# Moving the inverse of the 16-blocks and the decay chain of a gated DeltaNet branch, with new due times

## The chip, the cores and the metric

One core of one Trainium2 chip runs the whole program. The metric is the device time of one execution in microseconds (us); before the change the median of three runs is 1434.36 us (1434.13 to 1436.87). Five engines work side by side, each with an instruction queue of its own that runs in order: TensorE (PE in the profile; PEld is its weight load), VectorE (DVE), ScalarE (ACT), GpSimd (POOL) and SyncE (SP), which here only issues transfers.

## The reference

A trunk of two layers over 256 tokens of width 1024. Each layer has a mixing part with three branches, then a mixture of 32 experts:

```python
p = h @ w_in          # q,k,v of A and B; q,k,v,z and decay/beta of C; gates
ya = _global_gqa(...)             # rms norm, rotary, softmax attention, 8 heads
yb = _neighbourhood_attn(...)     # windowed attention, 4 heads
yc = _gdn_bidir(...)              # gated DeltaNet, 4 heads, forward and backward
mix = ga * (ya @ wa) + gb * (yb @ wb) + gc * (yc @ wc)
h = layernorm(alpha * h + mix @ w_out)
h = layernorm(alpha * h + moe(h))
```

Branch C convolves q, k and v along the tokens (5 taps), takes SiLU, and runs a chunked delta rule. Per chunk of 64 tokens:

```python
g = -exp(A_log) * softplus(a + dt_bias);  beta = sigmoid(b)
gc = cumsum(g);  decay = exp(gc_i - gc_j)
m = strict_lower(k_beta @ k.T) * decay
u, w = solve(m + I, [v * beta, k_beta * exp(gc)])   # unit triangular
# then a scan over the chunks with a state per head
```

## The kernel before

**Stages.** Each layer has a mixing part (`mixer`, about 0 to 260 and 714 to 967 us of the trace) and an expert part (`moe`). In mixing, weights come in units of 512 KB or less: SP loads a unit, ACT rounds it to its high half (uh), and VectorE, or POOL for the units listed in `POOL`, takes the low half (ul, "a cut", L189). Three products of halves stand for one exact product (`mm3`). `take` loads four to five units ahead and cuts three ahead. Expert weights come in slabs of 1 MB through the same SP queue; fifteen slots on the right side are shared with the tiles of the mixing part ("places" A to U, L147): a place that `free` gives back can take a slab. Seven more slots and one open on the left when the mixer's own tiles are gone.

**Order.** TensorE's order in mixing is pinned to the order of the program text. The text runs `projections` (ga0, cqk, cz, cv, akv, aq, ga1, bqk, bv, gb0, gb1, gc0, gc1), then `merge` a, b, c, then `project`. Beside it run side lines (generators): `delta_line`, `key_line`, `query_line`, `attention_line`, `router_line`. A clock of the kernel's own adds a planned time for each product (`mm`, `tp`). After each step of a projection `pump` runs each line whose due time has come. A line that yields is due again after the next number of its list in `LAGS` (L46). So LAGS alone decides where in TensorE's order the steps of a line stand. The order on the other engines is left to the tile framework's scheduler, except where `high_priority`, `manual_schedule` or `issue_after` binds it.

**The delta line** (L626 to L971). Step one computes gates: tanh of z into szg, beta, and the decay chain that gives g (`sc`, `sb`; L636 to L669, a softplus by a series), then three products R of g with triangles on POOL (L678), then convolution 2. After a lag of 15.03, step two: sums of g on TensorE into bank eb, their exponents ev, factors nbe and kds, and the three decay differences db with exponents E (L683 to L709). Then turned q and k (qk, L720), their norms with `rsqrt` (a first step on VectorE, a power on POOL, L238), turned v (vt), products kT, qdT, and the grams (gr, L778) from which VectorE makes Z and qk. The diagonal 16-blocks of Z are gathered into Zc (L797, L799), written to DRAM and read back as Zd with one block per partition (L804, L806). The inverse of each block takes 15 steps of two instructions on POOL (L812 to L817), a transposing copy (L818), then goes back over DRAM (L821, L824) into Wc. Sixteen masked POOL products (L830) make block-diagonal X and Y. After a lag of 53.51, the doublings on TensorE: T (T16), X and Y (X16, Y16), T3, L. Then the scan of four steps: ks, vn, kv, ob, and at the end ycT.

**Convolution** `conv(i, b)` (L555): for two halves a centre tap (L561) and four shifted taps on VectorE, tanh on ACT, one product into cs[i]. `conv(0)` and `conv(1)` follow cqk, `conv(2)` stands in the delta line.

**Rotary** `norm_rope` (L571): a copy from PSUM (queries), squares on ACT, sums on VectorE, `rsqrt`, then x times the root, then two POOL products with the sines, one with the cosines and the sum on VectorE. `key_line` uses it with a lag of 10.0 before its transposes (kTA), `query_line` with 16.22 (qTA).

**Attention.** `attention_line` starts when keys and queries are done: scores (s_a), `softmax` (maxima, factors and scaling on VectorE, exponents on ACT), transposes (pT_a), values (o_a), four pairs of heads; then two pairs of branch B.

Names in the trace: a tile inside a place bears the place's name (placeB holds big8, cy1 and cs0; placeF big5 and big6, that is X and Y; placeJ Zc, Zd and tmp; placeS the small ones). gap holds kT, g, ev and the like. A line such as L164, L168, L173 is that of a helper (`tt`, `ts`, `stt`).

## Time and profile before

| what | us |
|---|---|
| median of three runs | 1434.36 |
| the profiled execution's own time | 1437.54 |
| its span, first to last instruction | 1435.9 |
| TensorE busy | 1349.3 |
| VectorE busy | 613.6 |
| ScalarE busy | 399.2 |
| POOL busy | 256.5 |

The profiled execution is 3.2 us above the median, 1.6 of it outside the span. Times in the rows further below count from the span's start. A row of a timeline has the start, the duration, engine, line and operation, the tiles (out<-in), the shapes, the count of merged instructions, and in brackets the engine's idle time before it and what ended it. Matmuls are pipelined and their ends are modelled, so starts are surer than ends. PEclk is the granted TensorE clock as a share of 2.4 GHz. The table's busy times are totals over stretches with different limits; what a part costs is read from its own stretch.

### The profile page before, as it was taken

Reading aid. Unit: us, or ns where it says so; the run is one execution under the profiler, and the core shown is the slowest. Engines: PE = TensorE matmul, PEld = TensorE weight load, DVE = VectorE, ACT = ScalarE, POOL = GpSimd, SP = SyncE. Lnnn points to the kernel's source line nnn. Section 1 sums busy time; section 2 is a strip of 40 time slices with the busy share of each in tenths; the row PEclk is TensorE's granted clock in tenths of the full one; section 3 lists DMA queues with packets and bytes.
Section 4 is the critical chain, followed back from the end, with each engine's and each line's share of the span. In section 5 each row is a group of like instructions: output and inputs, shape, how many; then the busy total and the mean of one; then the engine's idle time right before and its main releaser. Section 6 shows DMA issues by size and latency. Waiting matters only on the chain. (4 is left out here: it accounts for less than half of the span.)

```text
span 1435.9 us, 23914 instructions
## 1 busy us (share of the span) xinstructions
PE 1349.3 (94%) x9788; PEld 894.9 (62%) x9788; DVE 613.6 (43%) x1221; ACT 399.2 (28%) x761; POOL 256.5 (18%) x327
## 2 busy tenths in 40 slices
PE   8989999899998999999898899999999899999986
PEld 7867777555555555555487877875555555555532
DVE  6887567522221222222279866773222122222214
ACT  4445543221111211111235365332111111111111
POOL 4474303300000000000046661132000000000000
PEclk9989999999999999999999999999999999999998
DMA  7635779799999999999856466787999999999994
GB/s 233 211 113 139 249 252 341 278 409 418 419 419 414 419 419 419 419 419 420 352 153 194 122 194 232 282 348 287 419 419 418 418 420 419 419 419 419 418 419 189
DMA packets 114533, 479.89 MB, mean 334 GB/s; under 512 B 25168, under 2 KB 38000, under 8 KB 65520
## 3 DMA queue, kind: packets, MB, share of 16 engines
q1 hardware_dynamic: 112464, 471.85, 84.1%
q0 software_dynamic: 1376, 5.24, 1.0%
q8 instruction: 81, 1.33, 0.4%
q10 hardware_dynamic: 576, 1.18, 0.2%
q14 instruction: 36, 0.29, 0.1%
HBM read 476.40 MB, written 1.84 MB: 333 GB/s over the span
## 5 line engine op out<-in xcount | busy, mean ns | idle before, releaser
L179 PE MATMUL h<-w,h 128*64 128x256 f32 x2016 | 231.8, 386 | 22.6 <-PEq L1413 11.3
L179 PEld LDWEIGHTS h<-w,h 128*64 128x64 f32 x2016 | 143.9, 139 | 101.8 <-issue 16.9
L173 DVE SCALAR_TENSOR_TENSOR hid<-gate,h 128x256 f32<-128x256 f32 x64 | 26.9, 421 | 407.2 <-ACT gate L1504 407.2
L173 DVE SCALAR_TENSOR_TENSOR op<-mo,rt,op 64x512 fp32r<-64x512 f32 x128 | 96.0, 750 | 223.3 <-ACT op L1535 222.4
L1535 ACT ACTIVATE op<-mo,rt 64x512 fp32r<-64x512 f32 x128 | 87.4, 683 | 313.0 <-PE mo L179 273.5
L179 PE MATMUL mo<-w,hidT 128*64 128x512 f32 x720 | 167.8, 595 | 3.6 <-DMA w<-in_w_dram 1.6
L164 POOL TENSOR_TENSOR W<-P,rt 128x128 f32<-128x128 f32 x64 | 24.2, 398 | 779.1 <-PE PT L185 704.4
L1504 ACT ACTIVATE gate<-h 128x256 f32<-128x256 f32 x64 | 24.5, 384 | 408.3 <-PE h L179 408.3
L179 PEld LDWEIGHTS mo<-w,hidT 128*64 128x64 f32 x720 | 51.3, 137 | 92.2 <-issue 80.1
L179 PE MATMUL h<-w,xg 128*64 128x256 f32 x864 | 97.1, 381 | 3.8 <-ACT h L1478 2.4
L179 PE MATMUL h<-wl,h 128*64 128x256 f32 x768 | 86.3, 381 | 2.2 <-ACT h L1478 1.4
L179 PEld LDWEIGHTS h<-w,xg 128*64 128x64 f32 x864 | 60.9, 137 | 36.0 <-ACT h L1478 3.8
L179 PEld LDWEIGHTS h<-wl,h 128*64 128x64 f32 x768 | 53.9, 137 | 30.6 <-ACT h L1478 2.4
L179 PE MATMUL mo<-wl,hidT 128*64 128x512 f32 x304 | 70.1, 597 | 2.9 <-DMA wl<-in_w_dram 2.9
L179 PE MATMUL my<-op,PT 128*128 128x512 f32 x256 | 69.6, 411 | 0.4 <-DVE op L173 0.3
L179 PEld LDWEIGHTS my<-op,PT 128*128 128x128 f32 x256 | 45.6, 188 | 22.1 <-issue 12.4
L179 PE MATMUL xg<-P,hh 128*128 128x256 f32 x256 | 54.8, 294 | 0.0
L179 PEld LDWEIGHTS xg<-P,hh 128*128 128x128 f32 x256 | 39.1, 188 | 24.6 <-issue 24.4
L179 PE MATMUL h<-wl,xg 128*64 128x256 f32 x416 | 48.3, 382 | 5.2 <-DMA wl<-in_w_dram 3.6
L179 PE MATMUL xg<-P,hl 128*128 128x256 f32 x256 | 51.1, 281 | 0.0
L179 PEld LDWEIGHTS mo<-wl,hidT 128*64 128x64 f32 x304 | 20.6, 136 | 38.0 <-issue 32.4
L179 PEld LDWEIGHTS h<-wl,xg 128*64 128x64 f32 x416 | 28.6, 137 | 22.7 <-DMA wl<-in_w_dram 6.8
(459 smaller groups left out, 2456.7 us busy)
## 6 DMA issues: line engine op xcount, KB each, us to landing
w<-in_w_dram SPq DMA_DIRECT2D x268, 1024.0 KB, 19.9
wl<-in_w_dram SPq DMA_DIRECT2D x112, 1024.0 KB, 19.9
w_gb<-in_w_in_dram SPq DMA_DIRECT2D x16, 512.0 KB, 3.5
w_gc<-in_w_in_dram SPq DMA_DIRECT2D x16, 512.0 KB, 4.6
w_wo<-in_w_out_dram SPq DMA_DIRECT2D x16, 512.0 KB, 4.4
w_ga<-in_w_in_dram SPq DMA_DIRECT2D x14, 512.0 KB, 5.6
w_cqk<-in_w_in_dram SPq DMA_DIRECT2D x8, 512.0 KB, 3.5
w_aq<-in_w_in_dram SPq DMA_DIRECT2D x8, 512.0 KB, 4.9
```

The source lines that it names most:

```text
L164: return eng.tensor_tensor(out=o, in0=x, in1=y, op=op).ins
L173: return V.scalar_tensor_tensor(out=o, in0=x, scalar=s, in1=y, op0=op0, op1=op1)
L179: ins = T.matmul(o, l, r, start=start, stop=stop, skip_group_check=True).ins
L1504: A.activation(g, b[:, :256], AF.Tanh, scale=0.5)
L1535: A.activation(hi, src, AF.Copy, scale=w)
```

## The change

Decay chain: it reads its inputs from PSUM, has fewer instructions (factors folded), multiplies by a negated exp(A_log) made beforehand on POOL, and makes the two halves of g itself; gates and beta come after it. `conv(2)` is bound to be issued behind it. The centre tap of each convolution goes from VectorE to ACT. The exponents of eb are written twice, also to PSUM, for nbe and kds. Rotary: raw x is copied and turned on POOL, the root's first step goes to POOL, and the root multiplies last. cs[0] is written straight to kq, so its copy on POOL goes; places D and E swap their order. Diagonal blocks: one scaling and three multiply-adds through PSUM. The inverse goes to VectorE, in order behind the last cut on VectorE, after a new yield; its transposing copy to ACT; X takes four ACT instructions and Y one on VectorE. Lags: 53.51 becomes 12.0 (to the inverse) and 20.0 (to the doublings), keys 10.0 to 14.0, queries 16.22 to 20.5. Lines of context are left out below.

```diff
@@ -44,9 +44,9 @@
-    "delta": [15.03, 1.23, 3.7, 10.0, 0, 0.76, 53.51, 0, 0, 0.8, 0.24, 0.0, 0.52, 1.67, 1.37, 0, 2.87, 2.23, 0, 2.03, 1.99, 0, 2.87, 1.99, 0, 2.87, 6.3],
-    "key": [10.0],
-    "query": [16.22, 1.92, 1.92],
+    "delta": [15.03, 1.23, 3.7, 10.0, 0, 0.76, 12.0, 20.0, 0, 0, 0.8, 0.24, 0.0, 0.52, 1.67, 1.37, 0, 2.87, 2.23, 0, 2.03, 1.99, 0, 2.87, 1.99, 0, 2.87, 6.3],
+    "key": [14.0],
+    "query": [20.5, 1.92, 1.92],
@@ -145,8 +145,8 @@
-              "C": {"big7": 1024, "cs2": 512, "cs1": 512}, "D": {"kd": 1024, "kq": 1024},
-              "E": {"qA": 1024, "ub": 768}, "F": {"big5": 1024, "big6": 1024},
+              "C": {"big7": 1024, "cs2": 512, "cs1": 512}, "E": {"qA": 1024, "ub": 768}, "D": {"kd": 1024, "kq": 1024},
+              "F": {"big5": 1024, "big6": 1024},
@@ -235,10 +235,10 @@
-    def rsqrt(o, x, scale, eps, n):
+    def rsqrt(o, x, scale, eps, n, eng=V):
...
-            ts(V, o, x, scale, OP.mult, eps, OP.add)
+            ts(eng, o, x, scale, OP.mult, eps, OP.add)
@@ -294,6 +294,8 @@
+            if i not in POOL:
+                scope["cut"] = made[1]
@@ -550,7 +552,7 @@
-        cs = [of(f"cs{i}", 2, S) for i in range(3)]
+        cs = [kq[:, 1]] + [of(f"cs{i}", 2, S) for i in (1, 2)]
@@ -558,7 +560,7 @@
-                ts(V, y[:, m], bv[:, m], cw[:, ch, 2:3], OP.mult)
+                A.activation(y[:, m], bv[:, m], AF.Copy, scale=cw[:, ch, 2:3])
@@ -572,25 +574,23 @@
-            xv = x8(x[:, :n * 64])
-            raw = x8(b) if which else xv
-            if not which:
-                A.copy(x[:, :n * 64], b)
-            sq = y
-            A.activation(sq[:, :n * 64], b if which else x[:, :n * 64], AF.Square)
+            xv, yv = x8(x[:, :n * 64]), x8(y[:, :n * 64])
+            A.copy(x[:, :n * 64], b)
+            A.activation(dst, x8(b) if which else xv, AF.Square)
             rs = of(f"rs{t}", 8)
-            V.tensor_reduce(out=rs[:, :n], in_=x8(sq[:, :n * 64]), axis=AX.X, op=OP.add)
-            rsqrt(rs[:, :n], rs[:, :n], 1.0 / 64.0, 1e-6, n)
-            tt(V, xv, raw, rs[:, :n, None].to_broadcast([128, n, 64]), OP.mult)
-            yv = x8(y[:, :n * 64])
+            V.tensor_reduce(out=rs[:, :n], in_=dst, axis=AX.X, op=OP.add)
+            rsqrt(rs[:, :n], rs[:, :n], 1.0 / 64.0, 1e-6, n, G)
...
+
+            xv = x8(b) if which else xv
             tt(V, xv, xv, gc_[:, which, 0, t:t + 1].to_broadcast([128, n, 64]), OP.mult)
-            tt(V, dst, xv, yv, OP.add)
+            tt(V, xv, xv, yv, OP.add)
+            tt(V, dst, xv, rs[:, :n, None].to_broadcast([128, n, 64]), OP.mult)
@@ -626,47 +626,44 @@
-            ba = of("ba", 2, 2, 2, 4)
-            for t in range(2):
-                V.tensor_copy(ba[:, :, :, t], zb[t][:, 256:272].rearrange("p (a d h) -> p a d h", a=2, d=2))
-                A.activation(szg[:, t], zb[t][:, :256], AF.Tanh, scale=0.5)
-                stt(szg[:, t], szg[:, t], 1.0, zb[t][:, :256], OP.add, OP.mult)
-            tt(G, szg.rearrange("p t (h d) -> p (t h) d", d=64), szg.rearrange("p t (h d) -> p (t h) d", d=64),
-               gn[:, 2:3].to_broadcast([128, 8, 64]), OP.mult)
+
+            sb = bank("s", f"sb{l}")
+            rr, sq_, acc, th_ = (sb[:, 16 * i:16 * i + 16] for i in range(4))
+            by_t = lambda ap: ap.rearrange("p (d t h) -> p d t h", d=2, t=2)
+            by_d = lambda ap: ap.rearrange("p (d h) -> p d h", d=2)
             beta = of("beta", 2, 8)
-            A.activation(beta, ba[:, 0].rearrange("p d t h -> p d (t h)"), AF.Tanh, scale=0.5)
-            ts(V, beta, beta, 0.5, OP.mult, 0.5, OP.add)
             sc = of("gsc", 8, 16)
-            av = ba[:, 1].rearrange("p d t h -> p (d t h)")
+            xx, ax, ee, ss, pp, g = (sc[:, i] for i in range(6))
...
-
-            def dh(ap8):
-
-                return ap8.rearrange("p (d h) -> p d h", d=2)[:, :, None, :].to_broadcast([128, 2, 2, 4])
-
-            xx, ax, ee, ss, pp, g = (sc[:, i] for i in range(6))
-
-            sb = bank("s", f"sb{l}")
-            rr, sq_, acc = (sb[:, 16 * i:16 * i + 16] for i in range(3))
-            tt(V, xx.rearrange("p (d t h) -> p d t h", d=2, t=2), ba[:, 1], dh(al[:, 1]), OP.add)
+            nea = sc[:, 6]
+            for t in range(2):
+                ts(G, by_t(nea)[:, :, t], by_d(ea), -1.0, OP.mult)
+            for t in range(2):
+                tt(V, by_t(xx)[:, :, t], by_d(zb[t][:, 264:272]), by_d(al[:, 1]), OP.add)
...
-            tt(V, ss, ee, rr, OP.mult)
-            tt(V, pp, sq_, ss, OP.mult)
+            stt(ss, ee, 2.0, rr, OP.mult, OP.mult)
+            stt(pp, sq_, 0.5, ss, OP.mult, OP.mult)
...
-            ts(V, xx, xx, 0.0, OP.max)
-            stt(acc, acc, 2.0, xx, OP.mult, OP.add)
-            tt(V, g.rearrange("p (d t h) -> p d t h", d=2, t=2), acc.rearrange("p (d t h) -> p d t h", d=2, t=2),
-               dh(ea), OP.mult)
-            ts(V, g, g, -1.0, OP.mult)
+            stt(acc, xx, 0.0, acc, OP.max, OP.add)
+            tt(V, g, acc, nea, OP.mult)
+            for c2 in range(2):
+                decayed = stt(sc[:, c2], acc, C("half")[:, c2:c2 + 1], nea, OP.mult, OP.mult).ins
+            for t in range(2):
+                A.activation(by_t(th_)[:, :, t], by_d(zb[t][:, 256:264]), AF.Tanh, scale=0.5)
+                A.activation(szg[:, t], zb[t][:, :256], AF.Tanh, scale=0.5)
+                stt(szg[:, t], szg[:, t], 1.0, zb[t][:, :256], OP.add, OP.mult)
+            tt(G, szg.rearrange("p t (h d) -> p (t h) d", d=64), szg.rearrange("p t (h d) -> p (t h) d", d=64),
+               gn[:, 2:3].to_broadcast([128, 8, 64]), OP.mult)
+            ts(V, beta, th_, 0.5, OP.mult, 0.5, OP.add)
@@ -678,26 +675,27 @@
-            conv(2, vbank)
+            with tc.issue_after(decayed):
+                conv(2, vbank)
...
-                ts(V, sc[:, c2], g, C("half")[:, c2:c2 + 1], OP.mult)
...
+            A.activation(eb[:, 64:128], eb[:, :64], AF.Exp)
...
-            edl = ev[:, 16:32].rearrange("p (d x) -> p d x", d=2)
+            egp, edl = (eb[:, 64 + 16 * i:80 + 16 * i].rearrange("p (d x) -> p d x", d=2) for i in range(2))
...
-                stt(nbe[hs, c], egc[hs, 0, t * 4:t * 4 + 4], -1.0, beta[hs, 0, t * 4:t * 4 + 4], OP.mult, OP.mult)
-                ts(V, nbe[hs, 3 - c], egc[hs, 1, t * 4:t * 4 + 4], -1.0, OP.mult)
+                stt(nbe[hs, c], egp[hs, 0, t * 4:t * 4 + 4], -1.0, beta[hs, 0, t * 4:t * 4 + 4], OP.mult, OP.mult)
+                ts(V, nbe[hs, 3 - c], egp[hs, 1, t * 4:t * 4 + 4], -1.0, OP.mult)
@@ -725,7 +723,7 @@
-                rsqrt(rk[:, t], rk[:, t], 1.0, 1e-6, 8)
+                rsqrt(rk[:, t], rk[:, t], 1.0, 1e-6, 8, G)
@@ -743,7 +741,8 @@
-                tt(V, vb[hs, c].rearrange("p (h d) -> p h d", d=64), vb[hs, 3 - c].rearrange("p (h d) -> p h d", d=64),
+                tt(V, vb[hs, c].rearrange("p (h d) -> p h d", d=64),
+                   b[hs, (1 - t) * 256:(2 - t) * 256].rearrange("p (h d) -> p h d", d=64),
@@ -761,7 +760,6 @@
-            G.tensor_copy(kq[:, 1], cs[0])
@@ -791,17 +789,18 @@
-            Zm = of("big8", 16, 4, 16)
...
-            tt(V, Zm.rearrange("p x b j -> p x (b j)"), Zf, C("bm16")[:, None, :].to_broadcast([128, 16, 64]), OP.mult)
             Zc = of("Zc", 16, 16)
-            V.tensor_reduce(out=Zc, in_=Zm.rearrange("p x b j -> p x j b"), axis=AX.X, op=OP.add)
+            part = bank("s", f"zc{l}")[:, :256].rearrange("p (x j) -> p x j", x=16)
+            ts(V, part, Zf[:, :, 0:16], bm[:, 0, 0:1], OP.mult)
+            for b_ in range(1, 4):
+                stt(Zc if b_ == 3 else part, Zf[:, :, 16 * b_:16 * b_ + 16], bm[:, b_, 0:1], part, OP.mult, OP.add)
+            d1 = dr.tile([16, 128, 16], F32, tag="d1", name=f"d1{l}")
+            SP.dma_start(d1.rearrange("x p j -> p x j"), Zc)
...
-            d1 = dr.tile([16, 128, 16], F32, tag="d1", name=f"d1{l}")
-            SP.dma_start(d1.rearrange("x p j -> p x j"), Zc)
@@ -809,13 +808,15 @@
-            for j in range(15):
-                n, m = 15 - j, j + 1
-                tv = tmp[:, :n * m].rearrange("p (i c) -> p i c", i=n)
-                tt(G, tv, Zd[:, j + 1:, j:j + 1].to_broadcast([128, n, m]),
-                   W0[:, j:j + 1, :m].to_broadcast([128, n, m]), OP.mult)
-                tt(G, W0[:, j + 1:, :m], W0[:, j + 1:, :m], tv, OP.subtract)
-            G.tensor_copy(Wd[:, 1], W0.rearrange("p i j -> p j i"))
+            yield
+            with tc.high_priority(offset=PRI), tc.manual_schedule(engines={V.engine}), tc.issue_after(scope["cut"]):
+                for j in range(15):
+                    n, m = 15 - j, j + 1
+                    tv = tmp[:, :n * m].rearrange("p (i c) -> p i c", i=n)
+                    tt(V, tv, Zd[:, j + 1:, j:j + 1].to_broadcast([128, n, m]),
+                       W0[:, j:j + 1, :m].to_broadcast([128, n, m]), OP.mult)
+                    tt(V, W0[:, j + 1:, :m], W0[:, j + 1:, :m], tv, OP.subtract)
+                A.copy(Wd[:, 1], W0.rearrange("p i j -> p j i"))
@@ -824,11 +825,10 @@
-            for w, o in ((1, Y), (0, X)):
-                for x0 in (0, 8):
-                    for b_ in range(4):
-                        tt(G, o[:, x0:x0 + 8, b_ * 16:b_ * 16 + 16], Wc[:, w, x0:x0 + 8],
-                           bm[:, b_:b_ + 1].to_broadcast([128, 8, 16]), OP.mult)
+            for b_ in range(4):
+                A.activation(X[:, :, b_ * 16:b_ * 16 + 16], Wc[:, 0], AF.Copy, scale=bm[:, b_, 0:1])
+            tt(V, Y.rearrange("p x (b j) -> p x b j", b=4), Wc[:, 1][:, :, None, :].to_broadcast([128, 16, 4, 16]),
+               bm[:, None].to_broadcast([128, 16, 4, 16]), OP.mult)
...

```

## Rows read from the trace of the kernel before

**Rows 1.** The page's head: the span, then busy time of each engine.

```profile
span 1435.9 us, 23914 instructions
...
PE 1349.3 (94%) x9788; PEld 894.9 (62%) x9788; DVE 613.6 (43%) x1221; ACT 399.2 (28%) x761; POOL 256.5 (18%) x327
```

**Rows 2.** Windows of 10 us: engines' busy us (instructions), PEclk, DMA share, GB/s.

```profile
270.00:280.00 10.00, 9.49 (x80) 6.50 (x80) 3.16 (x11) 1.40 (x4) 1.51 (x4) 1.00 0.38 109
...
290.00:300.00 10.00, 10.00 (x80) 5.43 (x78) 2.33 (x4) 1.67 (x4) 0.00 (x0) 1.00 0.99 418
```

**Rows 3.** TensorE's waits over both layers: us in total, times, longest us.

```profile
PE qTA L185 <- DVE placeE L164: 7.0, 2, 3.5
...
PE eb L179 <- DVE gap L168: 6.4, 2, 3.3
...
PE qTA L185 <- ACT placeI L772: 1.5, 2, 0.8
```

**Rows 4.** TensorE's timeline, first layer: start us, us, what, [idle before <-releaser].

```profile
70.87 1.77 PE L179 MATMUL eb<-gap,placeK 128*128 128x8 f32 x12 [3.05 <-DVE gap L168]
...
101.82 0.90 PE L185 MATMUL qTA<-cst,placeE 128*128 128x128 f32 x3 [3.53 <-DVE placeE L164]
...
105.21 1.89 PE L179 MATMUL gr<-placeD 64*64 64x128 f32 x32
...
111.93 1.14 PE L179 MATMUL s_a<-gap,placeA 64*128 64x256 f32 x8
...
122.72 0.55 PE L185 MATMUL pT_a<-cst,placeH 128*128 128x128 f32 x3 [0.59 <-DVE placeH L168]
...
155.77 1.15 PE L179 MATMUL T<-placeF,placeA 64*64 64x64 f32 x32
```

**Rows 5.** Windows around the two stops, first and second layer; columns as in rows 2.

```profile
67.40:78.00 10.60, 7.18 (x25) 3.73 (x25) 9.12 (x29) 3.06 (x8) 7.22 (x10) 0.84 0.50 150
78.00:94.00 16.00, 16.00 (x88) 13.71 (x87) 13.35 (x24) 11.03 (x17) 12.95 (x8) 1.00 0.27 84
...
102.00:107.00 5.00, 5.00 (x47) 4.57 (x46) 3.92 (x7) 1.21 (x2) 2.02 (x3) 0.51 0.42 107
...
774.00:785.00 11.00, 7.31 (x27) 4.17 (x26) 9.20 (x28) 3.49 (x10) 7.68 (x10) 0.84 0.49 146
...
809.00:814.00 5.00, 5.00 (x48) 4.60 (x49) 4.06 (x8) 1.20 (x2) 2.14 (x3) 0.56 0.39 109
```

**Rows 6.** VectorE's timeline, first layer: the decay chain's first steps and its last product.

```profile
51.48 0.18 DVE L164 TENSOR_TENSOR gap<-gap,placeS 128x16 f32<-128x16 f32 x1
...
51.90 1.17 DVE L168 TENSOR_SCALAR gap<-gap 128x16 f32<-128x16 f32 x1
...
70.38 0.17 DVE L164 TENSOR_TENSOR gap<-sb,gap 128x16 f32<-128x16 f32 x1
```

**Rows 7.** POOL's timeline: a cut; the inverse's first and last instruction (30); X and Y.

```profile
50.30 2.73 POOL L189 TENSOR_TENSOR ul_akv<-w_akv,uh_akv 128x512 fp32r<-128x512 f32 x2 [1.49 <-ACT uh_akv L189]
...
121.88 0.60 POOL L164 TENSOR_TENSOR placeJ<-placeJ,placeB 128x15 f32<-128x15 f32 x1 [9.80 <-DMA placeJ<-d]
...
137.18 0.22 POOL L164 TENSOR_TENSOR placeB<-placeB,placeJ 128x15 f32<-128x15 f32 x1
...
143.74 9.67 POOL L164 TENSOR_TENSOR placeF<-placeC,placeK 128x128 f32<-128x128 f32 x16 [4.54 <-DMA placeC<-d]
```

**Rows 8.** SP's timeline: the transfer that writes the diagonal blocks to DRAM.

```profile
115.80 0.37 SPq L804 DMA_DIRECT2D d<-placeJ  x1
```

**Rows 9.** SP's waits over both layers; columns as in rows 3.

```profile
SPq L824 <- DMA d<-placeB: 23.8, 2, 11.9
```

**Rows 10.** VectorE's groups from 40 to 112 us: what, xcount | busy us, mean ns.

```profile
L189 DVE TENSOR_TENSOR ul_ga<-w_ga,uh_ga 128x1024 fp32r<-128x1024 f32 x4 | 4.9, 1214 | 0.0
...
L173 DVE SCALAR_TENSOR_TENSOR placeA<-cv,placeS,placeA 128x254 f32<-128x254 f32 (+1 forms) x8 | 3.8, 470 | 0.0
...
L164 DVE TENSOR_TENSOR placeC<-placeB,gr 128x128 f32<-128x128 f32 x4 | 1.1, 283 | 0.7 <-PE gr L179 0.7
```

## The prediction

> **What bounds the kernel now.** I read the page first, then windows of 10 us, then TensorE's waits, then its timeline, and last the timelines of the engines that end those waits. The page [rows 1] says that TensorE (PE) is busy 94% of 1435.9 us, which alone says little: the two layers have two kinds of stretch. In the expert stretch the DMA engines are the limit: from 290 us on they are busy 0.99 of the time at 418 GB/s, but just before, from 270 to 280, only 0.38 [rows 2]. So every weight slot is full when the experts start, and the stream is paced from that moment. If the mixing part ends x us sooner, the experts start and end x us sooner, layer by layer. What has to be found is how long TensorE stands still in mixing.
>
> TensorE's order is written by hand, so a stop there delays all that follows. Its waits [rows 3] name two large ones in mixing, each once per layer: the decay sums (eb) wait 6.4 us in two visits for VectorE (DVE), and the turned queries (qTA) wait 7.0 for VectorE's last rotary sum and 1.5 before that for ScalarE (ACT). The timeline [rows 4] has them at 70.87 and 101.82 us. After each stop the granted clock is low [rows 5]: mean 0.84 from 67.4 to 78 (one short spell at half, 1.2 instead of 2.4 GHz), 0.51 from 102 to 107, and the same in the second layer (0.84 and 0.56). The doublings, whose first product T stands at 155.77 without idle time before it [rows 4], and the scan behind them make TensorE wait for nothing now.
>
> **What the change can give back.** The decay chain gives g late because it is interleaved with convolution 2: it starts at 51.48 and the product with exp(A_log) is issued at 70.38 [rows 6], 19 us for some 24 instructions of which a clean one takes 0.18. Behind it from now on stand the eight taps of convolution 2, 0.47 each [rows 10], 3.8 us, and two centre taps go to ACT. With these out of the way, and the two products with the halves folded into the chain, g comes 5 to 6 us sooner, more than the 3.05 us that eb waits [rows 4]. What is late next is db, which needs three POOL products of g; they move up with g. So eb's 6.4 us go, and the spells at low clock behind them: (1 - 0.84) x 10.6 = 1.7 us and (1 - 0.84) x 11 = 1.8 us of work lost [rows 5].
>
> The queries: with eb's stop and its slow spell gone the end of the projection aq, which stands behind them in the order, comes 3.05 + 1.7 us sooner, and qTA's lag rises from 16.22 to 20.5 of the kernel's clock. Working that clock through by hand puts qTA behind the grams (gr) instead of before them, one bqk step more away. The rotary's POOL products now read the raw x and need not wait for the root, and the root's scale comes last, so VectorE's wait for POOL's power lies beside the rotary. That is more than the 3.5 us missing. The 7.0 and 1.5 us go, with (1 - 0.51) x 5 = 2.4 and (1 - 0.56) x 5 = 2.2 us of clock.
>
> Sum over both layers: 6.4 + 1.7 + 1.8 + 7.0 + 1.5 + 2.4 + 2.2 = **23.0 us**. That is the ceiling. No matrix product is removed, and no transfer of weights.
>
> **What it adds.** Instructions that move between engines and shorten nothing TensorE waits for cost nothing while covered: centre taps to ACT, the root's first step to POOL, intermediates in PSUM, the copy of cs0 on POOL that goes. Their cover is thin on POOL: it is busy 12.95 of 16 us from 78 to 94 [rows 5], and the same work must fit a shorter stretch. If it doesn't, qTA waits again, between 0 and its present 4.2 us a layer. With PSUM holding more (the convolution's bank, sb, eb) a db product can wait for a bank: 0 to 1 us. I take 0.75 us a layer for the two, the lower part, because both have lost several us of other delay.
>
> The inverse is the large move. On POOL its 30 instructions run from 121.88 to 137.40, 15.5 us, and the 16 masked products of X and Y take 9.67 more [rows 7]. On VectorE a dependent small instruction follows the last in about 0.2 us (two steps from 51.48 to 51.90 [rows 6]); these have 15 to 64 elements, so 30 x 0.2 to 30 x 0.28 = 6 to 8.4 us, I take 7. X and Y become four ACT instructions and one on VectorE, an estimate of 1.9 us side by side, from VectorE's 0.47 for 256 elements [rows 10] taken for each of the four. The diagonal blocks are four more of that size, 1.9. The first trip over DRAM lasts from 115.80 to 121.88, 6.1 us [rows 7, 8]; the second, with the transposing copy, from 137.40 to 143.74, 6.3 [rows 7]. From the grams' end to X and Y: 16 products at 0.28, 4.5 at most, blocks 1.9, a cut of weights in between 1.2 [rows 10], first trip 6.1, inverse 7, copy and second trip 6.3, masks 1.9: 29 us, where it is 46 now (107.1 to 153.4 [rows 4, 7]).
>
> TensorE asks for them 48.7 us after the grams now (107.1 to 155.77, [rows 4]) for a lag of 53.51; the new lag of 12 + 20, worked through the clock to the step at which it falls due, is about 31 us. So about 2 us of slack, and T need not wait. The scan, moved up with it, ends before the merges; that saves nothing, since nothing waits for it now.
>
> But VectorE is then held. The block stands in order behind the last cut of weights and can start only when the first trip lands. Behind it wait that engine's cuts for gb and the softmax of the first two heads, whose transposes (pT_a) already wait 0.59 us at 122.72, 10.8 us after their scores at 111.93 [rows 4]. By the same clock VectorE has about 17 us from the grams to pT_a, and the work is 20 to 23: products and blocks 6.4, inverse 7, and an estimate of 7 to 9 for the cuts of bv and gb and the softmax. Some cuts can slip, since three units are cut ahead. I take 3.0 us a layer with its share of clock; the ends are 0 (all slips) and 7 + 2.4 (the whole inverse and a spell at half clock). The queue on SP holds too: it waits 11.9 us a layer for the second trip [rows 9] with gate weights behind it, and TensorE feels nothing of it today; nearer to gb I leave that at 0, with 3 us as the far end. ACT's transposing copy waits for the thirtieth instruction with casts and exponents behind it, in the same 3.0.
>
> Sum: 23.0 - 2 x (3.0 + 0.75) = 15.5 us. The profiled execution took 1437.54 us around its span of 1435.9, 3.2 above the median of 1434.36. From its own time that gives 1422.0, from the median **1419 us**.
>
> **The port rule.** One VectorE instruction of 128x16 at 51.90 took 1.17 us beside 0.18 for its neighbour at 51.48, while POOL worked through 50.30 to 53.03 [rows 6, 7]. The Trainium skill, SBUF — State Buffer, section "SBUF: two separate sides", says that VectorE and GpSimd share a port pair as an exclusive lock, which a VectorE instruction with two SBUF inputs needs too. This speaks against moving the inverse, and the trace agrees with it. By it 30 waits of 1 us would make the inverse 37 us, T would come 28 us late, and the time would be 1434.4 + 2 x (28 + 2.4 - 11.5) = 1472 us; I give it 0.02, in the chance of (b). The row against: POOL stood idle 9.80 us before 121.88 [rows 7], and the change leaves it there only two products with the lower blocks' mask.
>
> **The rivals.** (a) *VectorE is held where softmax is due.* The stalls go, but pT_a waits the whole 9.4 us a layer: 23.0 - 18.8 - 1.5 = 2.7, and half of that wait as the middle of the case: 23.0 - 9.4 - 1.5 = 12, so 1422 to 1432, I put it at 1428. For it: the 0.59 us. Against: the new step is emitted after those scores, and cuts have three units of lead. Chance 0.22.
>
> (b) *The doublings come before their inputs.* The place is T. If the chain stays near its present 46 us, because VectorE gives the inverse its turn late, TensorE stops 46 - 31 = 15 us and loses about 2.4 us of clock behind it, 17.4 against 11.5 gained per layer: 1434.4 + 2 x 5.9 = 1446 us. It decides from a chain of 31 + 11.5 - 2.4 = 40 us on, 11 above my sum. For it: the two trips are 12 us that no engine shortens. Against: the 15.5 and 9.67 us on POOL are most of the 46. Chance 0.13.
>
> (c) *Nothing arrives.* The stops move: VectorE is busy 9.12 of the 10.6 us around eb, and POOL in the row below [rows 5]. If either is the true pace, eb and qTA wait as long in other places: 1434 within 3 us. Against: taps, halves and the roots' first steps leave VectorE, and results in PSUM take the place of some that are stretched today (1.17 for 0.18 us, [rows 6]). Chance 0.10.
>
> **The numbers.** Forecast 0.55, at 1419. Below the ceiling's 1434.4 - 23.0 = 1411 there is only noise and unlisted small gaps: low end 1409. The high end takes in (a) and (c), 1437, and leaves (b) out. A measurement of this kernel can tell about 0.2%, 2.9 us, from no change. Faster by more: 0.55 + 0.22 = 0.77; within: 0.10; slower: 0.13.
>
> **What would show it.** Right: eb and qTA vanish from the waits, no low clock near 70 and 100 us, gr some 9 us sooner, the inverse on VectorE in 6 to 8 us, T without a wait some 31 us after the grams, and experts that start about 8 us sooner in the first layer and 16 in the second. Wrong: pT_a waiting several us for VectorE (a), T waiting for the masks (b), qTA still waiting for POOL or VectorE (c), or the transfers not full when the experts start, which would break the passing on.

## The result, and the profile after

The changed kernel takes 1459.9 us (median of 4 runs, 1458.71 to 1461.76) against 1435.61 for the kernel before beside it: ratio 1.0169, 95% interval 1.0154 to 1.0184. It is 24.3 us slower where 15.5 us less were forecast, and lies above the range.

The page's head, for [rows 1]:

```profile
span 1457.0 us, 23928 instructions
...
PE 1354.7 (93%) x9788; PEld 897.5 (62%) x9788; DVE 605.5 (42%) x1257; ACT 409.8 (28%) x791; POOL 204.4 (14%) x247
```

VectorE and POOL have less to do than before (605.5 for 613.6, 204.4 for 256.5), and the span is longer all the same: the time went into waits. TensorE's waits over both layers, for [rows 3]:

```profile
PE gr L179 <- DVE placeI L164: 6.9, 2, 3.4
PE aq L179 <- DVE placeG L173: 5.8, 2, 3.0
...
PE tpm L185 <- POOL mix L164: 5.8, 4, 1.6
PE pT_a L185 <- DVE placeJ L164: 4.4, 2, 2.4
...
PE bqk L179 <- DVE ul_bqk L189: 3.7, 2, 1.9
```

Both stops of [rows 3] are gone, eb and qTA, as forecast. Five others, larger than they were or new, stand there. TensorE's timeline in the first layer, for [rows 4]:

```profile
62.09 0.47 PE L179 MATMUL aq<-uh_aq,placeT 128*128 128x512 f32 x1 [3.04 <-DVE placeG L173]
...
72.63 1.41 PE L179 MATMUL eb<-gap,placeK 128*128 128x8 f32 x12
...
94.02 0.38 PE L179 MATMUL bqk<-placeT,ul_bqk 128*128 128x256 f32 x1 [1.86 <-DVE ul_bqk L189]
...
105.09 1.97 PE L179 MATMUL gr<-placeD 64*64 64x128 f32 x28 [3.43 <-DVE placeI L164]
...
142.79 1.15 PE L179 MATMUL T<-placeF,placeA 64*64 64x64 f32 x32
```

eb comes 1.8 us later than in [rows 4] although it no longer waits: aq's stop in front of it costs what eb's did. The grams end at 107.06, as before (107.1). T has moved from 155.77 to 142.79, 35.7 us behind the grams, and does not wait. Windows, columns as in [rows 2], around the new stops, at the merges and at the change to the experts; the fence behind them is the kernel before at the merges:

```profile
58.00:66.00 8.00, 4.96 (x17) 3.67 (x17) 5.44 (x14) 3.55 (x11) 7.84 (x5) 0.79 0.67 221
92.00:110.00 18.00, 12.71 (x106) 11.70 (x105) 16.61 (x39) 4.89 (x8) 7.75 (x6) 0.82 0.41 118
124.00:132.00 8.00, 5.95 (x25) 4.41 (x24) 7.02 (x24) 4.02 (x7) 0.36 (x1) 0.79 0.91 293
200.00:215.00 15.00, 14.05 (x76) 11.30 (x76) 8.64 (x13) 8.63 (x14) 1.66 (x1) 1.00 1.03 405
...
280.00:290.00 10.00, 9.56 (x76) 7.09 (x78) 4.94 (x14) 1.61 (x5) 3.34 (x6) 1.00 0.27 80
```

```profile
200.00:215.00 15.00, 15.00 (x138) 13.52 (x138) 9.14 (x20) 6.20 (x9) 1.67 (x1) 1.00 0.83 321
```

Each new stop has its spell at low clock: 0.79, 0.82 and 0.79, where the kernel before has 1.00, 0.81 and 1.00 in the same stretches; from 67.4 to 78 the clock is now 1.00 (0.84 in [rows 5]). The transfers still fall idle just before the experts (0.27 at 280 to 290; 0.38 ten us sooner in [rows 2]), and the loss passes on: in the profiled executions the first product of the ranking before the experts (rk) comes 12.1 us later in the first layer and 22.1 in the second. From 200 to 215 the DMA engines are full where they stood at 0.83, which the forecast did not have.

VectorE in the first layer: a cut and the gate behind it, a product held for a root, and the inverse between softmax and cuts; behind that TensorE at pT_a.

```profile
59.45 2.16 DVE L189 TENSOR_TENSOR ul_aq<-w_aq,uh_aq 128x1024 fp32r<-128x1024 f32 x1 [0.84 <-ACT uh_aq L189]
...
61.54 0.41 DVE L173 SCALAR_TENSOR_TENSOR placeG<-placeG,cz 128x256 f32<-128x256 f32 x1
...
90.41 0.42 DVE L164 TENSOR_TENSOR placeA<-qk,placeS 128x256 f32<-128x256 f32 x1 [6.56 <-POOL placeS L242]
...
117.51 0.18 DVE L164 TENSOR_TENSOR placeJ<-placeJ,placeB 128x15 f32<-128x15 f32 x1 [0.87 <-DMA placeJ<-d]
...
124.33 1.22 DVE L189 TENSOR_TENSOR ul_gb<-w_gb,uh_gb 128x1024 fp32r<-128x1024 f32 x1
...
127.13 0.35 DVE L168 TENSOR_SCALAR placeH<-placeH,placeS 128x256 f32<-128x256 f32 x1
...
131.16 0.17 DVE L164 TENSOR_TENSOR placeB<-placeB,placeJ 128x15 f32<-128x15 f32 x1
```

```profile
127.62 1.20 PE L185 MATMUL pT_a<-cst,placeH 128*128 128x128 f32 x4 [2.05 <-DVE placeJ L164]
```

POOL meanwhile, from the rotary's products to the root of k:

```profile
79.28 2.25 POOL L164 TENSOR_TENSOR placeH<-placeH,placeA 128x256 f32<-128x256 f32 x2 [1.14 <-ACT placeH L578]
81.49 2.33 POOL L164 TENSOR_TENSOR placeF<-placeF,placeK 128x512 f32<-128x512 f32 x1
...
85.31 1.66 POOL L242 TENSOR_TENSOR placeS<-placeS,mhalf 128x8 f32<-128x8 f32 x1
...
88.73 1.64 POOL L242 TENSOR_TENSOR placeS<-placeS,mhalf 128x8 f32<-128x8 f32 x1
```

The gate's first product runs at 61.54, and aq goes on 0.1 us after its end. The chain's last product had run at 58.25; between the two stands a cut of aq's weights that took 2.16 us beside work on POOL, where the cut of gb at 124.33 took 1.22. VectorE stands 6.56 us idle before 90.41: the product that scales kh (the normed keys of branch C) needs a root that waits on POOL behind rotary products, masks and the queries' root. The inverse runs from 117.51 to 131.33; the softmax's third scale, at 127.13, stands behind 18 of its 30 instructions and four cuts of gb, and 0.1 us after its end pT_a goes on.

### The profile page after: what moved, and what is told of

Same layout as the page of the kernel before. It is cut to its first block, busy times and chain, and to the rows that moved or that the text cites. A ratio compares the mean times of both kernels' runs of the same rounds, so it can differ in the third digit from the quotient of the medians.

```text
span 1457.0 us, 23928 instructions
## 1 busy us (share of the span) xinstructions
PE 1354.7 (93%) x9788; PEld 897.5 (62%) x9788; DVE 605.5 (42%) x1257; ACT 409.8 (28%) x791; POOL 204.4 (14%) x247
## 5 line engine op out<-in xcount | busy, mean ns | idle before, releaser
L179 PEld LDWEIGHTS h<-w,h 128*64 128x64 f32 x2016 | 143.7, 138 | 98.6 <-issue 13.7
L164 POOL TENSOR_TENSOR W<-P,rt 128x128 f32<-128x128 f32 x64 | 24.3, 400 | 778.0 <-PE PT L185 704.8
```

The source lines that it names most:

```text
L164: return eng.tensor_tensor(out=o, in0=x, in1=y, op=op).ins
L179: ins = T.matmul(o, l, r, start=start, stop=stop, skip_group_check=True).ins
```

## The experiments

Each time is set against the runs of the kernel before in the same comparison (1434.8 to 1436.3). No kernel leaves work out.

**The burst of slabs.** Expert slabs are fetched when places of the delta line become free.

```diff
-FREED = 1
+FREED = 0
```

> The changed kernel (1459.9 us), but a place that becomes free starts no expert slab by itself: slabs go only one by one beside a load of mixing weights. Theory 3, the burst: the delta line ends sooner and frees its places at once, nine expert slabs go ahead of the weights of the branches, and the merges and the last projection lose 5.1 us a layer. Then TensorE's excess from the first merge product on falls from 9.9 us to 5 to 6 a layer and the time is 1449 to 1454. Rival: the branch weights are late for another reason, or what is gained is paid at the experts, whose slabs come later: 1457 us or more.

Measured: 1452.74 us, ratio 1.0117 [1.0100, 1.0134], 6.9 us better than the change. Then the doublings' lag alone:

```diff
-    "delta": [15.03, 1.23, 3.7, 10.0, 0, 0.76, 12.0, 20.0,
+    "delta": [15.03, 1.23, 3.7, 10.0, 0, 0.76, 12.0, 41.5,
```

> The changed kernel (1459.9 us) with the doublings at their old place in TensorE's order (second lag 41.5 in place of 20), the inverse where the change put it. Theory 3 says that the sooner doublings and scan cost the waits in the scan (vn) and the 5.1 us a layer in the merges: 1446 to 1452 us with the waits of aq, gr and pT_a as they are. Rival: they cost nothing, and the merges are late because all of VectorE's and ACT's work before them is late: 1457 to 1462.

Measured: 1453.86, 1.0133 [1.0114, 1.0152], 5.8 better. Both together:

> The changed kernel with late doublings (1453.9 us) and slabs one by one (1452.7 us alone) together. If both take away the same loss, the burst of slabs in front of the branch weights, the two together give no more than the better alone: 1450 to 1455. If the sooner doublings cost something by themselves (the waits of vn, the order of the gc weights), they add: 1444 to 1448.

Measured: 1454.04, 1.0132 [1.0110, 1.0153]: one loss, removed either way. SP's timeline of the changed kernel shows it:

```profile
192.09 5.04 SPq L1295 DMA_DIRECT2D w<-in_w_dram  x4
197.22 0.39 SPq L285 DMA_DIRECT2D w_br0a<-in_w_branch_a_dram  x1
197.85 8.25 SPq L1295 DMA_DIRECT2D w<-in_w_dram  x2
206.19 0.99 SPq L285 DMA_DIRECT2D w_br0a<-in_w_branch_a_dram  x1
209.39 0.81 SPq L1295 DMA_DIRECT2D w<-in_w_dram  x2
210.29 0.90 SPq L285 DMA_DIRECT2D w_br0b<-in_w_branch_b_dram  x2
```

Eight slabs go out in 18 us, in front of w_br0b; one by one they alternate with the weights. "Since nothing waits for it now" was true of data; what follows the scan is the freeing of places, and that sets the order of the transfers.

**The two banks.** The gate in front of the chain again:

```diff
+            for t in range(2):
+                A.activation(by_t(th_)[:, :, t], by_d(zb[t][:, 256:264]), AF.Tanh, scale=0.5)
+                A.activation(szg[:, t], zb[t][:, :256], AF.Tanh, scale=0.5)
+                stt(szg[:, t], szg[:, t], 1.0, zb[t][:, :256], OP.add, OP.mult)
             with tc.issue_after(scope["turned"][0]):
```

> The changed kernel (1459.9 us) with one part undone: zb's gate (the two tanh and the two VectorE products) is taken before the decay chain again, not behind it. Theory 1, the bank: aq waits 5.8 us in two visits because the gate products, now behind the chain, hold the two accumulator banks of zb. Then aq's wait falls under 1 us, the spell at half clock behind it (62.7 us) goes, and the time is 1450 to 1454. Rival: the two products in front of the chain make g late again, eb waits some 3 us a layer in aq's place, and the time stays within 1456 to 1461.

Measured: 1462.75, 1.0188 [1.0169, 1.0207]. aq's wait is gone and eb waits 6.6 us in two visits: the rival, with a time a little above its range. And the products of vb from their copy:

```diff
-                   b[hs, (1 - t) * 256:(2 - t) * 256].rearrange("p (h d) -> p h d", d=64),
+                   vb[hs, 3 - c].rearrange("p (h d) -> p h d", d=64),
```

> The changed kernel (1459.9 us) with one part undone: the products of vb read the copy in SBUF again and not PSUM bank vt. Theory 2, the bank: the grams (gr) wait 6.9 us in two visits because VectorE holds vt until its products come. Then gr's wait falls under 1.5 us, the low clock behind it (103.7 to 110.5 us) goes, and the time is 1446 to 1452. Rival: VectorE is late in any case, behind POOL's root, and the wait only moves to the next product that needs VectorE (kT, qdT, the scores): 1457 to 1461.

Measured: 1459.84, 1.0171 [1.0148, 1.0194], no change. gr's 6.9 us go and gb (5.0) and qTA (3.5) wait instead: the rival again. In these two runs a bank decided which product waits, and the time did not fall.

**The rotary in the whole change**, put behind the root again with the roots' first step on VectorE, lags as changed; then with FREED = 0 besides:

```diff
-            rsqrt(rs[:, :n], rs[:, :n], 1.0 / 64.0, 1e-6, n, G)
+            rsqrt(rs[:, :n], rs[:, :n], 1.0 / 64.0, 1e-6, n)
+            tt(V, xv, raw, rs[:, :n, None].to_broadcast([128, n, 64]), OP.mult)
...
-            tt(V, xv, xv, yv, OP.add)
-            tt(V, dst, xv, rs[:, :n, None].to_broadcast([128, n, 64]), OP.mult)
+            tt(V, dst, xv, yv, OP.add)
...
-                rsqrt(rk[:, t], rk[:, t], 1.0, 1e-6, 8, G)
+                rsqrt(rk[:, t], rk[:, t], 1.0, 1e-6, 8)
```

> The changed kernel (1459.9 us) with the rotary behind the root again and the roots' first step on VectorE, as before. Theory 4, VectorE waits for POOL: in the changed kernel VectorE stands idle 4.5 us at 65 to 70 and 6.6 us at 84 to 90 us for POOL's rotary products and roots, in order, with taps, cuts and the products of vb behind it, and that is what makes bqk, gr and pT_a late. Then VectorE's idle time from 64 to 92 us falls from 11.6 to under 4 us, the waits of bqk and gr (1.9 and 3.4 in the first layer) fall under 1 together, aq's wait stays (its cause is the gate), and the time is 1444 to 1451. Rival: VectorE has too much to do in any case, the queries (qTA) wait again as in the kernel before, and the time is 1456 to 1462.

> The rotary behind the root as in the run before this one, and expert slabs only one by one beside loads. Theories 3 and 4 hold of different stretches, so the slabs' 7 us (1459.84 to 1452.74 alone) come on top: 1437 to 1444. Rival: they are the same lateness seen twice, and the two together give no more than 2 us over the better one alone.

Measured: 1463.97, 1.0203 [1.0180, 1.0225], and 1454.49, 1.0134 [1.0110, 1.0158]: 4.9 us above the change, and 2.3 above the slabs alone. So the rotary beside the root, with the roots' first step on POOL, is a gain in the whole change too, of some 5 us by the first pair and 2 by the second. Theory 4 in this form fell: VectorE's long wait is gone, but it waits 3.9 us for the key's root, which stands on POOL behind the three products of g that the sooner chain has put there, a cut and the gate's product; db (7.2) and gr (7.4) wait.

**The inverse back on POOL**, first with the rotary behind the root and late doublings, then with late doublings only:

```diff
-            with tc.high_priority(offset=PRI), tc.manual_schedule(engines={V.engine}), tc.issue_after(scope["cut"]):
+            if True:
...
-                    tt(V, tv, Zd[:, j + 1:, j:j + 1].to_broadcast([128, n, m]),
+                    tt(G, tv, Zd[:, j + 1:, j:j + 1].to_broadcast([128, n, m]),
...
-                    tt(V, W0[:, j + 1:, :m], W0[:, j + 1:, :m], tv, OP.subtract)
+                    tt(G, W0[:, j + 1:, :m], W0[:, j + 1:, :m], tv, OP.subtract)
```

and in the second also

```diff
-                A.copy(Wd[:, 1], W0.rearrange("p i j -> p j i"))
+                G.tensor_copy(Wd[:, 1], W0.rearrange("p i j -> p j i"))
```

> The rotary behind the root, and also the inverse on POOL and the doublings late, as before: of the change only the decay chain in front of convolution 2, the gate behind it, results in PSUM, the masks of X and Y and the two lags are left. If the stops of the inverse part are the pT_a wait (2.0 us a layer and its slow spell) and the merges' 5.1 us a layer, the time is 11 to 14 us under that of the rotary alone, 1431 to 1439. Rival: what is left still makes VectorE late before 110 us and its stops outweigh those that went (eb, qTA): 1440 us or more.

> The changed kernel with late doublings (1453.9 us), and the 30 instructions of the inverse and its transposing copy on POOL again. Rival (a) of the prediction says that pT_a (2.2 us in the first layer, with a slow spell) waits because VectorE holds the inverse: that stop falls under 1 us and the time is 1445 to 1450. Against it: the stop is the softmax being late behind the stops before it, and the time stays within 1451 to 1456.

Measured: 1475.76, 1.0277 [1.0253, 1.0301], and 1480.79, 1.0326 [1.0302, 1.0351]. Both are inconclusive on the inverse and telling on queues. In the first the transposing copy had stayed on ACT, which held a cast for it (gb waits 15.7 us in two visits). In the second, with that copy on POOL too, VectorE waits for the second trip, a softmax behind it:

```profile
138.42 1.23 DVE L164 TENSOR_TENSOR placeF<-placeC,placeK 128x1024 f32<-128x1024 f32 x1 [14.60 <-DMA placeC<-d]
```

This second run also shows what the move itself is worth. The first and the last of the 30 instructions on POOL:

```profile
117.34 0.22 POOL L164 TENSOR_TENSOR placeJ<-placeJ,placeB 128x15 f32<-128x15 f32 x1 [5.70 <-DMA placeJ<-d]
...
130.86 0.22 POOL L164 TENSOR_TENSOR placeB<-placeB,placeJ 128x15 f32<-128x15 f32 x1
```

There the inverse lasts 13.7 us, on VectorE in the change 13.8 (117.51 to 131.33). VectorE's instructions are shorter (0.17 to 0.23 us; POOL's 0.21 to 0.40, and three of 1.29 to 1.36), but softmax and cuts stand between them. So the inverse ends at the same time on either engine, and VectorE's mask product behind the second trip starts at 138.42 in both.

**The inverse behind the softmax**, still on VectorE, T at the same place:

```diff
-    "delta": [15.03, 1.23, 3.7, 10.0, 0, 0.76, 12.0, 41.5,
+    "delta": [15.03, 1.23, 3.7, 10.0, 0, 0.76, 22.0, 31.5,
```

> The changed kernel with late doublings (1453.9 us), the inverse issued 10 us later, so that VectorE has the first two heads' softmax ahead of it. Rival (a) of the prediction: pT_a's stop (2.2 us in the first layer, 2.6 in the second, with a slow spell of 3.4 us) goes, and if nothing takes its place the time is 1446 to 1450. Otherwise the next heads' softmax, or the gate weights behind the second trip on SP, wait as long: 1452 to 1458.

Measured: 1445.91, 1.0070 [1.0051, 1.0088], 8.0 us better than late doublings alone, with pT_a at 1.0 us in two visits (4.6 there). Rival (a)'s mechanism is shown. Its price is less sure: in the two profiled executions 3.2 us of the difference stand before the grams' end, ahead of the inverse (aq waits 3.2 us there in place of 5.3), although in the first layer VectorE, ACT and POOL run the same instructions in the same order up to there. So 8.0 us is the upper end of the price; without that part the profiled executions differ by 6.6.

**Each part alone on the kernel before.** The core of each edit; its other lines are those of the change. Decay chain, gate, convolution and eb:

```diff
-            conv(2, vbank)
+            with tc.issue_after(decayed):
+                conv(2, vbank)
```

Rotary, roots and the two lags:

```diff
-    "key": [10.0],
-    "query": [16.22, 1.92, 1.92],
+    "key": [14.0],
+    "query": [20.5, 1.92, 1.92],
...
+            rsqrt(rs[:, :n], rs[:, :n], 1.0 / 64.0, 1e-6, n, G)
```

Blocks, inverse, masks of X and Y, cs0 in place D and doublings:

```diff
-    "delta": [15.03, 1.23, 3.7, 10.0, 0, 0.76, 53.51,
+    "delta": [15.03, 1.23, 3.7, 10.0, 0, 0.76, 12.0, 20.0, 0,
...
+            with tc.high_priority(offset=PRI), tc.manual_schedule(engines={V.engine}), tc.issue_after(scope["cut"]):
```

> The kernel before (1434.8 us) with the decay part of the change alone: the chain in front of convolution 2 and the gate behind it, centre taps on ACT, the exponents of eb in PSUM. Theory 1, the wait changes places: eb's 3.05 us a layer go and aq waits some 3 us a layer for the gate in their place, and the half clock with it: 1431 to 1441. Rival: the part is good by itself and only the other parts spoil it: 1422 to 1429.

> The kernel before (1434.8 us) with the rotary part alone: rotary beside the root, the roots' first step on POOL, key lag 14 and query lag 20.5. Theory 4: qTA's stop (4.3 us a layer and 2.3 of clock) goes, but VectorE waits for POOL's roots with bqk's cuts behind it, so at most half arrives: 1428 to 1438. Rival: the part works as it was meant: 1419 to 1426.

> The kernel before (1434.8 us) with the inverse part alone: diagonal blocks and inverse on VectorE, masks of X and Y on ACT and VectorE, doublings at lag 12 + 20. Theory 3 and rival (a) of the prediction: pT_a waits 2 to 2.4 us a layer and its spell at half clock follows, and the burst of slabs costs the merges some 5 us a layer, with no stop taken away: 1446 to 1456. Rival: in the kernel before VectorE has room for it, and the cost is in how it meets the other parts: 1434 to 1440.

Measured: 1435.49 (0.9993 [0.9983, 1.0003]), 1447.32 (1.0078 [1.0058, 1.0097]), 1470.50 (1.0233 [1.0210, 1.0256]). The first lies in its range, the other two above all that was expected. In the first aq's 7.0 us in two visits stand for eb's 6.4, and qTA keeps 6.3 of its 8.5. In the third the keys wait 11.8 us, T 4.6 and pT_a 5.8. The three add to 45 us, the whole is 24: they do not add, and the keys' stop in the third, which the whole doesn't have, was not followed further. (None of the three has the products of vb from PSUM, which cost nothing above.)

**Lags alone.** On the kernel before, all three later, then the queries' alone:

```diff
-    "delta": [15.03,
+    "delta": [18.5,
-    "key": [10.0],
-    "query": [16.22, 1.92, 1.92],
+    "key": [14.0],
+    "query": [20.5, 1.92, 1.92],
```

> The kernel before (1435.3 us) with nothing but later places in TensorE's order: decay sums lag 18.5 in place of 15.03, keys 14 in place of 10, queries 20.5 in place of 16.22. If the two stops (eb 3.05, qTA 3.5 us a layer, with the half clock behind each) are only a matter of asking too soon, they go without any work moved: 1418 to 1426. Rival: VectorE and POOL are the pace there, the wait moves to the next product that needs them (db, gr, s_a), or the doublings and the scan, later by as much, run into the merges: 1432 to 1440.

> The kernel before (1434.8 us) with one number changed: queries at lag 20.5 in place of 16.22. If qTA's stop (4.3 us a layer, 2.3 of clock) is only a matter of asking too soon it goes, and nothing takes its place: 1422 to 1428. Rival: VectorE is the pace, and the grams, which now come first, wait as long: 1432 to 1438.

Measured: 1460.14, 1.0170 [1.0150, 1.0189], and 1452.21, 1.0109 [1.0078, 1.0140]. Both lie above all that was expected: here asking later cost more than the waits that it moved. TensorE's waits with the queries' lag alone:

```profile
PE gr L179 <- POOL placeD L764: 7.0, 2, 4.1
...
PE pT_a L185 <- DVE placeH L168: 4.9, 4, 2.5
```

qTA is gone, and the grams, now first, wait for POOL's copy of cs0. The rotary part without its lags:

```diff
-    "key": [14.0],
-    "query": [20.5, 1.92, 1.92],
+    "key": [10.0],
+    "query": [16.22, 1.92, 1.92],
```

> The rotary part alone (1447.3 us with its lags) with the old lags, key 10 and query 16.22: the kernel before (1435.4 us) with nothing but the rotary beside the root and the roots' first step on POOL. If the later places of the queries and keys are what costs, the time falls to 1427 to 1436, at or under the kernel before. If the rotary's work itself makes VectorE and POOL late, qTA's stop stays or grows (over 5 us a layer) and the time is 1440 us or more.

Measured: 1431.64, 0.9976 [0.9965, 0.9986], against 1447.32 with them: the rotary beside the root gains 4.7 us, its lags lose 15.8. Where: with the lags the attention falls later in TensorE's order, SP has no gc unit in front of the second trip, and all eight stand behind it. SP's timeline with the old lags, then SP's, ACT's and VectorE's of the rotary part alone:

```profile
125.77 0.37 SPq L285 DMA_DIRECT2D w_gc<-in_w_in_dram  x1
...
139.70 13.52 SPq L285 DMA_DIRECT2D w_gc<-in_w_in_dram  x7
```

```profile
136.99 1.48 SPq L822 DMA_DIRECT2D placeC<-d  x2
138.56 18.87 SPq L285 DMA_DIRECT2D w_gc<-in_w_in_dram  x8
```

```profile
143.81 1.05 ACT L189 CAST uh_gc<-w_gc 128x1024 fp32r<-128x1024 f32 x1 [7.40 <-DMA w_gc<-in_w_in_dram]
```

```profile
144.89 3.30 DVE L189 TENSOR_TENSOR ul_gc<-w_gc,uh_gc 128x1024 fp32r<-128x1024 f32 x1 [8.94 <-ACT uh_gc L189]
```

VectorE waits 8.94 us for that cast with a softmax behind it, and TensorE 4.2 for pT_a. A second trace of the lags is a wait of the doublings (L) for ACT, of 3.6 to 3.7 us in four visits. It stands in every run with the queries at 20.5, the delta line's first lag at 15.03 and the doublings at their old place, and in no run with the old lags. The change with late doublings and the inverse behind the softmax has it too:

```profile
PE L L179 <- ACT placeC L867: 3.6, 4, 1.5
```

**The banks freed without VectorE.** The decay part alone, zb copied out by ACT, and a cut of aq off POOL:

```diff
-POOL = (1, 2, 5, 13, 14, 15, 17, 18, 21, 23, 50, 62)
+POOL = (1, 2, 5, 13, 14, 15, 17, 18, 21, 50, 62)
+            raw = [of(n, 256) for n in ("Zc", "Zd")]
+            for t in range(2):
+                A.copy(raw[t], zb[t][:, :256])
+                A.activation(szg[:, t], zb[t][:, :256], AF.Tanh, scale=0.5)
+                A.activation(by_t(th_)[:, :, t], by_d(zb[t][:, 256:264]), AF.Tanh, scale=0.5)
-                stt(szg[:, t], szg[:, t], 1.0, zb[t][:, :256], OP.add, OP.mult)
+                stt(szg[:, t], szg[:, t], 1.0, raw[t], OP.add, OP.mult)
```

> The kernel before (1436.2 us) with the decay part alone (1435.5 us, aq waiting 3.4 us for the gate), but ACT copies zb to SBUF and takes the tanh ahead of the chain's end, so that the two accumulator banks are free without VectorE; and the fourth unit of aq is cut on VectorE, because on POOL it stands behind the three products of g. Theory 1, the bank: aq's stop is gone (under 0.5 us), TensorE reaches 92 us some 5 us sooner, and the time is 1426 to 1432, the part that qTA does not take back. Rival: the banks don't matter, aq or db waits as long for VectorE's or POOL's next late product: 1434 us or more.

Measured: 1440.98, 1.0047 [1.0031, 1.0063]. Theory 1 holds of the stop, aq and eb wait no more; of the time its rival holds:

```profile
PE qTA L185 <- DVE placeE L164: 13.7, 4, 6.8
PE kTA L185 <- ACT placeG L604: 5.5, 2, 2.7
```

And the same with the rotary beside the root, its first step on POOL, old lags:

```diff
-            rsqrt(rs[:, :n], rs[:, :n], 1.0 / 64.0, 1e-6, n)
-            tt(V, xv, raw, rs[:, :n, None].to_broadcast([128, n, 64]), OP.mult)
+            rsqrt(rs[:, :n], rs[:, :n], 1.0 / 64.0, 1e-6, n, G)
...
-            tt(V, dst, xv, yv, OP.add)
+            tt(V, xv, xv, yv, OP.add)
+            tt(V, dst, xv, rs[:, :n, None].to_broadcast([128, n, 64]), OP.mult)
```

> The run with zb copied out (1441.0 us, qTA waiting 6.5 us) and the rotary beside the root with the roots' first step on POOL for the rotary alone, lags as before. If the rotary's chain POOL, VectorE, POOL is what qTA waits for, it gets some 3 us shorter a layer: 1431 to 1436. If VectorE's and POOL's whole load sets the time there, qTA or the grams wait as long as they did: 1439 to 1444.

Measured: **1426.73 us, ratio 0.9933 [0.9910, 0.9956]**, faster than both kernels, better than expected, and 14.5 us under the run before it. TensorE's waits:

```profile
PE qTA L185 <- DVE placeE L164: 8.6, 4, 3.5
```

eb, aq, db and gr do not wait. When the queries' stop ends in the first layer tells more than its length: in the decay part alone, with zb copied out, and in this last run:

```profile
101.66 0.90 PE L185 MATMUL qTA<-cst,placeE 128*128 128x128 f32 x3 [3.16 <-DVE placeE L164]
...
105.19 0.90 PE L185 MATMUL qTA<-cst,placeE 128*128 128x128 f32 x3 [0.91 <-DVE placeE L164]
...
96.83 0.72 PE L185 MATMUL qTA<-cst,placeE 128*128 128x128 f32 x3 [3.52 <-DVE placeE L164]
```

Before the change it ends at 101.82 [rows 4]. Without eb's stop it ends no sooner; without eb's and aq's it ends 3.4 us later (that run also puts a cut on VectorE and two copies on ACT); with the rotary beside the root it ends 5 us sooner.

## Why the prediction was wrong

**By its steps.** Late doublings, then the inverse behind the softmax, split the 24.3 us: 5.8 for the doublings sooner, up to 8.0 for the inverse ahead of the softmax, and at least 10.5 left for all the rest, which is the decay part, the rotary part with its lags, and what stays of the inverse part (blocks, masks, cs0, the inverse on VectorE). Alone on the kernel before, the decay and the rotary part cost -0.7 and 11.2. That makes the same 10.5, but the three parts alone don't add to the whole, so the agreement may be luck.

- **The ceiling was the mis-sized term, and the step that failed.** The forecast had 23.0 - 1.5 = 21.5 us of gain from the decay and rotary parts; what is left of the change costs 10.5, an error of 32.0. "Eb's 6.4 us go" came true and gave nothing. The sum takes eb and qTA as two losses, each paid back when its stop goes. The runs show one pace behind both, VectorE's and POOL's work up to the queries: without eb's stop qTA's ends at 101.66 us in place of 101.82, and the decay part alone gives 0.7 us (within its noise) in place of eb's 9.9 with its clock. With eb and aq both out of the way qTA waits 13.7 us in place of 7.0. In the change the grams, forecast some 9 us sooner, end where they did. The queries' own work made shorter did give time back: 4.7 us for the rotary alone with the old lags, 14.5 in the last run. This is the mechanism of rival (c), the stops move, which had a chance of 0.10; its 1434 us leaves out what the lags, the slabs and the inverse cost.
- **The lags, counted as a gain.** "One bqk step more away" was read as slack for the queries. It also moves the attention, SP's order and the grams: 15.8 us in the rotary part alone, more than all of the 10.5. No run takes the lags alone out of the whole change, so their share there stays open; the wait of L for ACT is one part that can be seen.
- **Moved behind, costed at nothing.** The gate behind the chain had no line in the forecast. Its products release the accumulator banks that aq needs; that is aq's stop, and the copies on ACT removed it. The Trainium skill, Perfetto Trace Analysis, section "Optimization Strategy", says that the same gap repeating can mean there isn't enough SBUF or PSUM for the next tile. aq's stop (5.8 us in two visits) comes only once a layer, but it is of this kind, a wait for a bank. The runs also show a limit: the gate first and vb from its copy took such waits away and gained nothing.
- **POOL's thin cover** (0.75 us a layer) was the right place and too small. From 78 to 94 us POOL is busy 13.74 of 16 us (12.95 before, [rows 5]), though it has less to do in the whole, and the order there decides who waits: the root of k stands behind the rotary's products and the queries' root, 6.56 us of idle VectorE in one wait.
- **The inverse**: each of the 30 instructions takes 0.17 to 0.23 us as forecast, but the whole takes 13.8 us, not 7, with softmax and cuts in between, and ends no sooner than on POOL. T comes without a wait all the same. VectorE held: up to 8.0 us for the 6.0 put down. Rival (a) was right in kind.
- **The scan sooner, "saves nothing"**: it cost 5.8, through places freed sooner.
- **SP's queue at 0** held in the change itself (9.0 us of waits for the second trip, 23.8 in [rows 9]) and failed in the rotary part alone.

The errors: 32.0 + 2.0 + 5.8 = 39.8 us, the distance between -15.5 and 24.3; with a smaller price for the inverse the first grows by as much. What the 10.5 us are made of inside the whole change was not taken apart further: aq, bqk, gr and db (3.2, 3.8, 6.9 and 4.9 us with the inverse behind the softmax) moved among each other in every trial. Rival (b) did not occur. Its port rule was not put to the test, since POOL stood idle while VectorE's small instructions ran at 0.2 us; and the row that was taken for it, 51.90 in [rows 6], reads one tile of SBUF, not two.

## What to carry to other kernels

Two stops in a row on one hand-ordered engine can be one late chain: add their lengths only after asking what the second waits for once the first is gone. When a step is moved, list what its end releases (banks, places that start transfers) and whose queue it then holds, besides who reads its result. Asking for a result later was not free slack here, it cost 15.8 us: change lags by themselves, and measure them by themselves. And before moving a chain to a faster engine, count what that engine runs in between: 30 instructions that were shorter one by one ended at the same time.

## What the runs showed of the hardware

POOL's power (the root's second step) took 0.70 us for two columns and 1.64 for eight, more than its product of 512 elements at 76.17 us, so a small root can hold POOL's queue longer than a large product. And where both engines work, one can be stretched: VectorE's product of 512 elements at 79.70 us took 1.23 us, a like one 0.69 at 78.49 and 0.68 at 79.10, and POOL's at 81.49 took 2.33, 1.27 at 76.17. Not every such pair was: VectorE's cut at 81.45, beside that POOL product, took its usual 1.21.

```profile
78.49 0.69 DVE L164 TENSOR_TENSOR placeF<-placeF,placeK 128x512 f32<-128x512 f32 x1
79.10 0.68 DVE L164 TENSOR_TENSOR placeB<-placeB,placeS 128x512 f32<-128x512 f32 x1
79.70 1.23 DVE L164 TENSOR_TENSOR placeF<-placeF,placeS 128x512 f32<-128x512 f32 x1
```

```profile
72.17 0.70 POOL L242 TENSOR_TENSOR placeS<-placeS,mhalf 128x2 f32<-128x2 f32 x1
76.17 1.27 POOL L164 TENSOR_TENSOR placeB<-placeB,placeK 128x512 f32<-128x512 f32 x1 [3.31 <-ACT placeB L707]
```
